# Summing the second sublayer's shift and scale over partitions: one-column TensorE products, or VectorE block transposes with small transfers

## Chip, core and metric

The kernel runs on one core of one Trainium2 chip. The metric is the device time of one execution in microseconds (us), the median of several runs. A profiled execution has a time of its own, and its instructions are counted from the first to the last (the span).

## What is computed

The reference is one post-norm layer of a streaming encoder over 512 tokens of width 1024, with two sublayers. Each sublayer's input is a layer norm that is shifted and scaled by vectors made from a condition `c` of width 1024:

```python
c_act = jax.nn.silu(c)
mod = c_act @ w_ada[l] + b_ada[l]
sh_t, sc_t, gt_t, sh_f, sc_f, gt_f = jnp.split(mod, 6, axis=-1)
h = _modulate(x, sh_t, sc_t)          # _layer_norm(x) * (1 + sc) + sh
y = _token_mixer(h, ...)              # pooling, latent attention, spatial gating; gates; w_o
x = _layer_norm(ALPHA * x + gt_t[:, None, :] * y) * ln_t_g[l] + ln_t_b[l]
h = _modulate(x, sh_f, sc_f)          # the vectors that this change is about
y = _conv_ffn(h, ...)
x = _layer_norm(ALPHA * x + gt_f[:, None, :] * y) * ln_f_g[l] + ln_f_b[l]
```

The change concerns only how `sh_f` and `sc_f`, 1024 numbers each, get their last sum.

## The kernel before

Activations stand transposed in SBUF: eight tiles of 128 channels by 512 tokens. Every large product is made of float32r matmuls of 128x128 by 128x512 with each operand split in a high and a low part. `chunk` loads one 128x1024 piece of weights, ScalarE casts it to the high part (L92, tiles such as `wbh`), VectorE subtracts to get the low part (L93, `wbl`), and `mm_chunk` runs 16 products with the high part (L113, L114) and 8 with the low part (L116). High and low tiles have two buffers each, raw tiles three, and `chunk` prepares one piece ahead, so the cast for the piece after the next waits until TensorE has finished with the high part in use.

The modulation vectors are formed piece by piece during the mixer. `ada_piece(idx, k)` loads 128 rows of the matrix for vector `idx` (0: `gt_t`, 1: `sh_f`, 2: `sc_f`, 3: `gt_f`) in two halves `adar` and adds them, times the condition's value for each row, to two accumulators `acc` of 128x512 (L850, L852, on VectorE). After eight pieces `acc` holds, per output channel, 128 partial sums that lie on 128 partitions; they still have to be added over the partitions. `ada_cols` does this on TensorE: each of eight 128x128 blocks of `acc` is the stationary operand and a column of ones the moving one, so that the result lands as one column with channels on partitions (L879, tile `pmc`); VectorE adds the bias (L883) and, for the scale, one (L885). The results `shfc` and `scfc` are read by `second_modulation` (L1262 to L1270) when the second sublayer begins.

The program around this, in order: `uv_half(1, "v", ...)` (the second half of the gating branch's v, with the last four pieces of `sh_f`), then `ada_cols(1, ...)`, then the branch `merge(1, m)` for m = 0 to 7 with `v_stats` and `v_norm` hung behind the weight splits, then `gated(g)` for g = 0 to 7 with the pieces of `sc_f` (each `gated` ends with four small products `pz`, L1046), then `ada_cols(2, ...)`, four `gate(2, m)`, and `merge(2, m)` for m = 0 to 7, each of the first four followed by `gate(2, m + 4)`. In `merge(2, m)` VectorE forms `th` from the product (L414), GpSimd adds it to the merged tile `mg` (L417), and ScalarE and VectorE split that into `mgh` and `mgl` (L1080, L1081). GpSimd also multiplies six tiles `oraw` of the output projection by `gt_t` (L1077); these tiles share a pool of eight (`pt`) with `acc`, `adar` and `gt_t`. The output projection `project_out`, the norm, the second modulation and the gated MLP follow.

A scheduler sets the order of each engine's queue from the order in the program and from when buffers come free; `behind_split` (called with a function) holds that function's instructions behind the last low-part subtraction. SyncE's queue (SP) issues the loads, GpSimd's queue (POOL) issued none.

Of the kernel before, what the change touches and what calls it, by code (L numbers as in the profile page):

```python
# [8 lines left out]
F32 = mybir.dt.float32  # L9
# [3 lines left out]
ALU = mybir.AluOpType  # L13
AX = mybir.AxisListType

P = 128
S = 512
D = 1024
KT = 8
# [13 lines left out]
C_SHT, C_SCT, C_SHF, C_SCF = 8, 16, 24, 32  # L33
# [17 lines left out]
def trunk(ctx: ExitStack, tc: tile.TileContext, A, out):  # L51
    nc = tc.nc

    const = ctx.enter_context(tc.tile_pool(name="const", bufs=1))
# [2 lines left out]
    wp = ctx.enter_context(tc.tile_pool(name="wp", bufs=2))  # L57
    sm = ctx.enter_context(tc.tile_pool(name="sm", bufs=4))
    pp = ctx.enter_context(tc.tile_pool(name="pp", bufs=8, space=bass.MemoryType.PSUM))

    def ps(name):
        return pp.tile([P, 512], F32, name=name, tag="ps")

    def act_t(name, dt=F32R):
        return sb.tile([P, 512], dt, name=name, tag="act", bufs=48)
# [4 lines left out]
    def m_t(name, dt=F32):  # L70
        return sb.tile([P, 512], dt, name=name, tag="m", bufs=8)
# [4 lines left out]
    def pad_t(name, dt=F32):  # L76
        return pd.tile([P, 528], dt, name=name, tag="pad")

    def f(ap):
        return ap.bitcast(F32)  # L80
# [20 lines left out]
    def behind_split(work, *args):  # L101
        with tc.issue_after(last_lo[0]):
            work(*args)
# [6 lines left out]
    def mm_chunk(o, wh, wl, xh, xl):  # L110
        cs = [slice(k * P, (k + 1) * P) for k in range(KT)]
        for k, c in enumerate(cs):
            nc.tensor.matmul(o, wh[:, c], xl[k], start=k == 0, stop=False)  # L113
            nc.tensor.matmul(o, wh[:, c], xh[k], start=False, stop=False)  # L114
        for k, c in enumerate(cs):
            nc.tensor.matmul(o, wl[:, c], xh[k], start=False, stop=k == KT - 1)  # L116
# [39 lines left out]
    def row_tiles(r, alloc, name):  # L156
        ts = []
        for n in range(2):
            t = alloc(f"{name}{n}", F32)
            nc.sync.dma_start(  # L160
                out=t, in_=A["rows"][r : r + 1, n * 512 : (n + 1) * 512].broadcast_to([P, 512])
            )
            ts.append(t)
        return ts
# [3 lines left out]
    cols = const.tile([P, N_COLS], F32, name="cols")  # L168
# [4 lines left out]
    for t in range(TT):  # L173
        for n in range(2):
            x_load = (nc.scalar if t == 3 else nc.sync).dma_start(
                out=xs[t][n], in_=A["x"][t * P : (t + 1) * P, n * 512 : (n + 1) * 512]
# [4 lines left out]
    ones = const.tile([P, P], F32, name="ones")  # L181
# [180 lines left out]
    def chunk(key):  # L362
        if key not in plan:
            return wsplit(A[key[0]][key[1:]], D, key[0])
        i = used[0]
        assert plan[i] == key
        for j in (i, i + 1):
            if j < len(plan) and j not in split:
                split[j] = wsplit(A[plan[j][0]][plan[j][1:]], D, plan[j][0])
        used[0] += 1  # L370
        return split[i]
# [21 lines left out]
    def gate(b, m, pg=None):  # L393
        if pg is None:
            gh, gl = chunk(("wg", b * KT + m))
            pg = ps("pg")
            mm_chunk(pg, gh, gl, hT_hi, hT_lo)
        th = act_t(f"th{b}{m}", F32)
        nc.scalar.activation(th, pg, AF.Tanh, scale=0.5)
        return th  # L400
# [3 lines left out]
    def merge(b, m, bh, bl, th):  # L404
        yh, yl = chunk(("wb", b * KT + m))
        py = ps("py")
        mm_chunk(py, yh, yl, bh, bl)
        if b == 0:
            merged[m] = m_t(f"mg{m}")
            nc.vector.scalar_tensor_tensor(  # L410
                out=merged[m], in0=th, scalar=1.0, in1=py, op0=ALU.add, op1=ALU.mult
            )
        else:
            nc.vector.scalar_tensor_tensor(  # L414
                out=th, in0=th, scalar=1.0, in1=py, op0=ALU.add, op1=ALU.mult
            )
            nc.gpsimd.tensor_tensor(out=merged[m], in0=merged[m], in1=th, op=ALU.add)  # L417
# [160 lines left out]
    for t in range(TT):  # L578
# [4 lines left out]
        for dst, tab in ((tA, cosT), (tB, sinT)):  # L583
            nc.vector.tensor_tensor(
                out=dst[:, t, :].rearrange("p (a b) -> p a b", a=2), in0=src,
                in1=tab[:, t : t + 1, :].broadcast_to([P, 2, 32]), op=ALU.mult,
# [253 lines left out]
    ada_state = {}  # L840
# [16 lines left out]
    def ada_rows(idx, r, name):  # L857
# [13 lines left out]
            nc.vector.tensor_tensor(out=bias[n], in0=pg, in1=bias[n], op=ALU.add)  # L871
        return bias

    def ada_cols(idx, c0, one, name):
        acc = ada_state.pop(idx)
        dst = const.tile([P, KT], F32, name=name + "c")
        pm = ps("pmc")
        for j in range(KT):
            nc.tensor.matmul(  # L879
                pm[:, j : j + 1], acc[j // 4][:, (j % 4) * P : (j % 4 + 1) * P], ones[:, 0:1],  # L880
                start=True, stop=True,
            )
        nc.vector.tensor_tensor(out=dst, in0=pm[:, 0:8], in1=cols[:, c0 : c0 + 8], op=ALU.add)  # L883
        if one:
            nc.vector.tensor_scalar_add(out=dst, in0=dst, scalar1=1.0)  # L885
        return dst


    po_hi = [None] * KT
    po_lo = [None] * KT  # L890
# [50 lines left out]
    for g in range(4):  # L941
        if g % 2 == 0:
            wh, wl = chunk(("wpool", g // 2))
        for mo in range(2):
            m = 2 * g + mo
            pm = ps("pmx")
            for k in range(2):
                o = (g % 2) * 512 + k * 256 + mo * P
                c = slice(o, o + P)
# [8 lines left out]
    def uv_half(i, nm, hook=None):  # L958
        tiles = [act_t(f"{nm}{i}{t}", F32) for t in range(TT)]
        pu = [ps("pu") for _ in range(TT)]  # L960
        for q in range(4):
            wh, wl = chunk(("wsg", i, q))
            for rest in range(2):
                for t in range(TT):
                    ts_ = slice(t * P, (t + 1) * P)
                    for kk in range(2):
                        k = 2 * q + kk
                        c = slice(kk * 512, (kk + 1) * 512)
                        hh, hl = hT_hi[k][:, ts_], hT_lo[k][:, ts_]
                        if rest:  # L970
                            nc.tensor.matmul(pu[t], hh, wl[:, c], start=False, stop=k == KT - 1)
                        else:
                            nc.tensor.matmul(pu[t], hl, wh[:, c], start=k == 0, stop=False)
                            nc.tensor.matmul(pu[t], hh, wh[:, c], start=False, stop=False)  # L974
            if hook:
                hook(q)
        for t in range(TT):
            nc.scalar.activation(tiles[t], pu[t], AF.Gelu)
        return tiles
# [7 lines left out]
    v0 = uv_half(0, "v", lambda q: behind_split(ada_piece, 1, q))  # L987
    gt_t = ada_rows(0, 0, "gtt")
    v1 = uv_half(1, "v", lambda q: behind_split(v_second, q))
    shf = ada_cols(1, C_SHF, False, "shf")  # L990
    gsg = row_tiles(6, pt_t, "gsg")
    bsg = row_tiles(7, pt_t, "bsg")

# [16 lines left out]
        )  # L1010

    v_work = [[(v_stats,)]] + [[(v_norm, t, 0)] for t in range(4)]
    v_work += [[(v_norm, 0, 1), (v_norm, 1, 1)], [(v_norm, 2, 1)], [(v_norm, 3, 1)]]
    for m in range(KT):
        th = th1[m] if m < len(th1) else gate(1, m)
        merge(1, m, mx_hi, mx_lo, th)
# [10 lines left out]
    for n in range(2):  # L1027
        nc.gpsimd.affine_select(
            out=ws[n].rearrange("p (g t) -> p g t", g=4),
            in_=wsr[:, n * 512 : (n + 1) * 512].rearrange("p (g t) -> p g t", g=4),  # L1030
# [30 lines left out]

    for g in range(KT):
        gated(g)
    scf = ada_cols(2, C_SCF, True, "scf")
    th2 = {m: gate(2, m) for m in range(4)}
    mg_hi = []
    mg_lo = []
# [4 lines left out]
            nc.sync.dma_start(out=o_raw[k][n], in_=A["wo"][k, :, n * 512 : (n + 1) * 512])  # L1072
    for m in range(KT):
        merge(2, m, sg_hi, sg_lo, th2.pop(m))
        if m < 6:
            raw = o_raw[2 + m // 2][m % 2]
            nc.gpsimd.tensor_tensor(out=raw, in0=raw, in1=gt_t[m % 2], op=ALU.mult)  # L1077
        mh = act_t(f"mgh{m}")
        ml = act_t(f"mgl{m}")
        nc.scalar.activation(mh, merged[m], AF.Copy, scale=0.5)  # L1080
        nc.vector.scalar_tensor_tensor(  # L1081
            out=ml, in0=merged[m], scalar=0.5, in1=f(mh), op0=ALU.mult, op1=ALU.subtract
        )
        mg_hi.append(mh)
        mg_lo.append(ml)
        if m + 4 < KT:
            th2[m + 4] = gate(2, m + 4)


    lntg = row_tiles(2, act_t, "lntg")  # L1090
    lntb = row_tiles(3, act_t, "lntb")

# [231 lines left out]
    for t in range(TT):  # L1324
        x1[t] = [m_t(f"x1_{t}{n}") for n in range(2)]
        for n in range(2):
            nc.sync.dma_start(
                out=x1[t][n], in_=A["x"][t * P : (t + 1) * P, n * 512 : (n + 1) * 512]
# [41 lines left out]
    for i in range(NP):  # L1370
        half = []
        for v in range(2):
            m = 2 * i + v
# [4 lines left out]
            else:  # L1378
# [9 lines left out]
                out=t[:, 1:512], in0=pz[:, 0:511], scalar=cols[:, cc + 1 : cc + 2],  # L1388
                in1=t[:, 1:512], op0=ALU.mult, op1=ALU.add,
            )  # L1390
            nc.vector.scalar_tensor_tensor(  # L1391
                out=t[:, 2:512], in0=pz[:, 0:510], scalar=cols[:, cc : cc + 1],
                in1=t[:, 2:512], op0=ALU.mult, op1=ALU.add,
# [165 lines left out]
```

## Time and profile before

| quantity | us |
|---|---|
| median of 3 runs (lowest, highest) | 957.66 (957.44, 957.80) |
| span of the profiled execution | 956.3 |
| TensorE matmuls busy | 942.2 |
| VectorE busy | 584.9 |
| ScalarE busy | 380.3 |
| GpSimd busy | 284.1 |

The profiled execution's own time is taken as its span, 956.3 us; the median of the runs lies 1.4 us above that (launch and close of the program, which the span does not hold). In the rows below a timeline row is: start in us, duration in us, engine, line, operation, written tile and read tiles, shape, count, and in brackets the engine's idle time before the row with what ended it. PE is TensorE, PEld its weight loads, DVE VectorE, ACT ScalarE, POOL GpSimd, SPq the queue of SyncE. The granted TensorE clock is 0.999 of full speed.

### The profile page before, as it was taken

The page shows a single profiled execution, that of the slowest core. Times are in us where ns is not written, and L with a number is a line of the kernel's source. Part 1 is how long each engine was busy: PE and PEld are TensorE (multiplying, and loading weights), DVE is VectorE, ACT ScalarE, POOL GpSimd, SP SyncE. Part 2 cuts the span into 40 slices and gives each one's busy share as a digit, 9 for nine tenths or more (in the row PEclk, how much of TensorE's full clock was granted, in tenths as well). Part 3 has the DMA queues.
Part 4 walks back from the last instruction along what each step waited for, and adds up shares of the span by engine and source line. Part 5 has one row for each costly group of instructions (what it writes and reads, how often), then busy time and mean ns, then how long its engine had stood idle before and what let it go on. Part 6 is the DMA issues. An engine that isn't in the chain of part 4 may idle for free.

```text
span 956.3 us, 12108 instructions
## 1 busy us (share of the span) xinstructions
PE 942.2 (99%) x4556; PEld 795.5 (83%) x4556; DVE 584.9 (61%) x850; ACT 380.3 (40%) x623; POOL 284.1 (30%) x248
## 2 busy tenths in 40 slices
PE   7999999999999999999999999999999999999996
PEld 6988888888888888888888888988888888888885
DVE  7966767546786665567233589575565664623258
ACT  4575555533233322232322334644434444321121
POOL 4741121122440032202123713021111121756653
PEclk9999999999999999999999999999999999999999
DMA  9823202145436533554333540134334333432322
GB/s 324 318 72 100 62 31 83 45 132 154 135 111 216 181 118 109 181 182 141 124 110 114 165 162 24 60 118 131 110 119 140 115 119 102 129 114 88 91 86 89
DMA packets 46139, 119.72 MB, mean 125 GB/s; under 512 B 5504, under 2 KB 8960, under 8 KB 46080
## 3 DMA queue, kind: packets, MB, share of 16 engines
q1 hardware_dynamic: 45648, 118.39, 38.4%
q8 instruction: 36, 0.59, 0.2%
q10 hardware_dynamic: 432, 0.55, 0.2%
q14 instruction: 23, 0.19, 0.1%
HBM read 116.83 MB, written 2.10 MB: 124 GB/s over the span
## 4 chain that ended last, share of the span: by engine, by line
PE 86%; DMA 5%; DVE 5%; POOL 2%; issue 1%; ACT 1%; SPq 0%; POOLq 0%; DVEq 0%; ACTq 0%
PE pzu L114 7%; PE pzu L116 7%; PE pzu L113 7%; PE pg L113 4%; PE pg L114 4%; PE pg L116 4%; PE py L113 4%; PE py L114 4%; PE py L116 4%; PE pyd L1132 3%; PE pyd L1129 3%; PE pyd L1131 3%; DMA ada<-in_ada1p 2%; PE pu L114 2%; PE pu L113 2%; PE pu L974 2%
## 5 line engine op out<-in xcount | busy, mean ns | idle before, releaser
L93 DVE TENSOR_TENSOR wupl<-wup,wuph 128x1024 fp32r<-128x1024 f32 x38 | 47.8, 1257 | 71.8 <-PE pzu L116 45.9
L1098 POOL TENSOR_TENSOR d<-d,gtfb 128x512 f32<-128x512 f32 x44 | 73.7, 1697 | 38.1 <-DMA d<-in_wdn 36.5
L1402 POOL TENSOR_TENSOR zc<-zc 128x512 f32<-128x512 f32 x22 | 29.7, 1350 | 173.1 <-ACT zc L1401 130.8
L1103 DVE TENSOR_TENSOR dl<-d,dh 128x1024 fp32r<-128x1024 f32 x18 | 27.8, 1542 | 57.0 <-PE pyd L1129 51.9
L92 ACT CAST wuph<-wup 128x1024 fp32r<-128x1024 f32 x38 | 39.9, 1049 | 46.8 <-PE pzu L114 46.8
L417 POOL TENSOR_TENSOR mg<-mg,th 128x512 f32<-128x512 f32 x16 | 31.3, 1959 | 86.4 <-DVE th L414 86.4
L92 ACT CAST wbh<-wb 128x1024 fp32r<-128x1024 f32 x24 | 25.2, 1052 | 74.0 <-PE py L114 55.3
L852 DVE SCALAR_TENSOR_TENSOR ada<-adar,cact,ada 128x512 f32<-128x512 f32 x56 | 49.1, 907 | 1.8 <-DMA adar<-in_ada 1.8
L93 DVE TENSOR_TENSOR wgl<-wg,wgh 128x1024 fp32r<-128x1024 f32 x22 | 29.6, 1343 | 29.7 <-PE pg L116 14.9
L1102 ACT CAST dh<-d 128x1024 fp32r<-128x1024 f32 x18 | 18.9, 1052 | 62.5 <-PE pyd L1132 33.2
L1384 ACT ACTIVATE zc<-pzu,cols 128x512 f32<-128x512 f32 x44 | 34.1, 778 | 21.8 <-PE pzu L116 17.4
L93 DVE TENSOR_TENSOR wbl<-wb,wbh 128x1024 fp32r<-128x1024 f32 x24 | 30.6, 1275 | 14.9 <-ACT wbh L92 6.5
L771 POOL TENSOR_SCALAR pe<-pe,mx 128x128 f32<-128x128 f32 (+3 forms) x32 | 17.0, 533 | 69.3 <-DVE mx L770 52.4
L1387 DVE SCALAR_TENSOR_TENSOR zc<-pzu,cols,zc 128x511 f32<-128x511 f32 x44 | 32.6, 744 | 4.2 <-ACT zc L1384 4.2
L92 ACT CAST wgh<-wg 128x1024 fp32r<-128x1024 f32 x22 | 23.3, 1058 | 25.6 <-PE pg L114 19.8
L1391 DVE SCALAR_TENSOR_TENSOR zc<-pzu,cols,zc 128x510 f32<-128x510 f32 x44 | 32.6, 745 | 0.8
L414 DVE SCALAR_TENSOR_TENSOR th<-th,py 128x512 f32<-128x512 f32 x16 | 11.0, 687 | 35.6 <-PE py L116 35.6
L1401 ACT ACTIVATE zc<-zc 128x512 f32<-128x512 f32 x22 | 13.9, 631 | 40.5 <-DVE zc L1391 40.4
L905 POOL TENSOR_TENSOR asum<-apad 128x527 f32<-128x527 f32 x8 | 12.3, 1544 | 54.6 <-ACT apad L900 28.0
L296 DVE SCALAR_TENSOR_TENSOR acc<-ada,cact,acc 128x256 f32<-128x256 f32 (+1 forms) x29 | 27.4, 944 | 1.2 <-DMA ada<-in_ada1p 0.3
L1077 POOL TENSOR_TENSOR oraw<-oraw,gttb 128x512 f32<-128x512 f32 x6 | 10.5, 1775 | 47.3 <-DMA oraw<-in_wo 47.3
L1098 POOL TENSOR_TENSOR o<-o,gttb 128x512 f32<-128x512 f32 x10 | 17.4, 1757 | 13.5 <-DMA o<-in_wo 7.7
(1473 smaller groups left out, 3088.4 us busy)
## 6 DMA issues: line engine op xcount, KB each, us to landing
wup<-in_wup SPq DMA_DIRECT2D x44, 512.0 KB, 3.6
adar<-in_ada SPq DMA_DIRECT2D x64, 256.0 KB, 4.1
wb<-in_wb SPq DMA_DIRECT2D x24, 512.0 KB, 3.6
wg<-in_wg SPq DMA_DIRECT2D x22, 512.0 KB, 3.6
d<-in_wdn SPq DMA_DIRECT2D x22, 512.0 KB, 3.6
ada<-in_ada1p SPq DMA_DIRECT2D x24, 256.0 KB, 4.9
wa<-in_wa SPq DMA_DIRECT2D x8, 512.0 KB, 3.6
wsg<-in_wsg SPq DMA_DIRECT2D x8, 512.0 KB, 3.6
```

The source lines that it names most:

```text
L92: nc.scalar.copy(out=hi[:, :n], in_=raw[:, :n])
L93: ins = nc.vector.tensor_tensor(out=lo[:, :n], in0=raw[:, :n], in1=f(hi[:, :n]), op=ALU.subtract)
L113: nc.tensor.matmul(o, wh[:, c], xl[k], start=k == 0, stop=False)
L114: nc.tensor.matmul(o, wh[:, c], xh[k], start=False, stop=False)
L116: nc.tensor.matmul(o, wl[:, c], xh[k], start=False, stop=k == KT - 1)
L417: nc.gpsimd.tensor_tensor(out=merged[m], in0=merged[m], in1=th, op=ALU.add)
L852: nc.vector.scalar_tensor_tensor(out=acc[n], in0=src, scalar=cact[:, k : k + 1], in1=acc[n], op0=ALU.mult, op1=ALU.add,)
L1098: nc.gpsimd.tensor_tensor(out=halves[n], in0=halves[n], in1=gt[n], op=ALU.mult)
L1384: nc.scalar.activation(t, pz, AF.Identity, bias=cols[:, cc + 3 : cc + 4], scale=cols[:, cc + 2 : cc + 3])
L1387: nc.vector.scalar_tensor_tensor(out=t[:, 1:512], in0=pz[:, 0:511], scalar=cols[:, cc + 1 : cc + 2], in1=t[:, 1:512], op0=ALU.mult, op1=AL ...
L1391: nc.vector.scalar_tensor_tensor(out=t[:, 2:512], in0=pz[:, 0:510], scalar=cols[:, cc : cc + 1], in1=t[:, 2:512], op0=ALU.mult, op1=ALU.add,)
L1402: nc.gpsimd.tensor_tensor(out=val, in0=val, in1=gate, op=ALU.mult)
```

## The change

The sixteen one-column products are taken out. `ada_parts` instead transposes `acc` in 32x32 blocks on VectorE, so that the 32 partitions of a block come to lie along the free axis, and reduces them; what is left is, for each channel, four partial sums, one from each quarter of the partitions, spread over four groups of 32 partitions. They are written to a DRAM tile by one transfer and read back by four (one for each group of 32 channels), all issued by GpSimd, so that channels lie on partitions with four values each. `ada_cols` then reduces four values and adds the bias on VectorE. `ada_parts` for the shift stands behind the last `v_norm` in `merge(1, 7)`, for the scale in `merge(2, 1)`; the two `ada_cols` stand in `merge(2, 0)` and `merge(2, 5)`.

```diff
+    def ada_parts(idx, name):
+        acc = ada_state.pop(idx)
+        part = const.tile([P, 4, KT], F32, name=name + "p")
+        for n in range(2):
+            blocks = pad_t("adab")
+            nc.vector.transpose(out=blocks[:, :512], in_=acc[n])
+            nc.vector.tensor_reduce(
+                out=part.rearrange("p a j -> p j a")[:, 4 * n : 4 * n + 4, :],
+                in_=blocks[:, :512].rearrange("p (j a c) -> p j a c", a=4, c=32),
+                op=ALU.add, axis=AX.X,
+            )
+        bounce = dr.tile([P, 4, KT], F32, name=name + "d")
+        nc.gpsimd.dma_start(out=bounce, in_=part)
+        quarters = const.tile([P, 4, KT], F32, name=name + "q")
+        for a in range(4):
+            nc.gpsimd.dma_start(
+                out=quarters[32 * a : 32 * a + 32],
+                in_=bounce.rearrange("(q c) a j -> c q a j", c=32)[:, :, a, :],
+            )
+        ada_quarters[idx] = quarters
...
     def ada_cols(idx, c0, one, name):
-        acc = ada_state.pop(idx)
         dst = const.tile([P, KT], F32, name=name + "c")
-        pm = ps("pmc")
-        for j in range(KT):
-            nc.tensor.matmul(
-                pm[:, j : j + 1], acc[j // 4][:, (j % 4) * P : (j % 4 + 1) * P], ones[:, 0:1],
-                start=True, stop=True,
-            )
-        nc.vector.tensor_tensor(out=dst, in0=pm[:, 0:8], in1=cols[:, c0 : c0 + 8], op=ALU.add)
+        nc.vector.tensor_reduce(
+            out=dst, in_=ada_quarters.pop(idx).rearrange("p q j -> p j q"), op=ALU.add, axis=AX.X
+        )
+        nc.vector.tensor_tensor(out=dst, in0=dst, in1=cols[:, c0 : c0 + 8], op=ALU.add)
...
-    shf = ada_cols(1, C_SHF, False, "shf")
...
-    v_work += [[(v_norm, 0, 1), (v_norm, 1, 1)], [(v_norm, 2, 1)], [(v_norm, 3, 1)]]
+    v_work += [[(v_norm, 0, 1), (v_norm, 1, 1)], [(v_norm, 2, 1)], [(v_norm, 3, 1), (ada_parts, 1, "shf")]]
...
-    scf = ada_cols(2, C_SCF, True, "scf")
...
     for m in range(KT):
         merge(2, m, sg_hi, sg_lo, th2.pop(m))
+        if m == 1:
+            behind_split(ada_parts, 2, "scf")
+        if m == 0:
+            behind_split(ada_cols, 1, C_SHF, False, "shf")
+        if m == 5:
+            behind_split(ada_cols, 2, C_SCF, True, "scf")
```

How the queues change is seen at three places. First, VectorE's queue in `merge(1, 7)`, where `v` is normalised, `th` is the last product's gate and `wul` the first low parts of the `gated` stage. Before:

```order
L93 TENSOR_TENSOR wul<-wu,wuh 128x1024
L1005 SCALAR_TENSOR_TENSOR v_3217<-v_3217,mvv,gsg_3385 128x512
L1008 SCALAR_TENSOR_TENSOR v_3217<-v_3217,rsv,bsg_3389 128x512
L414 SCALAR_TENSOR_TENSOR th_3746<-th_3746,py 128x512
L93 TENSOR_TENSOR wul<-wu,wuh 128x1024
```

The same place in the changed program, whose lines stand one to twenty-seven lower:

```order
L94 TENSOR_TENSOR wul<-wu,wuh 128x1024
L1025 SCALAR_TENSOR_TENSOR v_3217<-v_3217,mvv,gsg_3376 128x512
L880 STREAM_TRANSPOSE adab<-ada_3074 128x512
L880 STREAM_TRANSPOSE adab<-ada_3075 128x512
L1028 SCALAR_TENSOR_TENSOR v_3217<-v_3217,rsv,bsg_3380 128x512
L881 TENSOR_REDUCE shfp<-adab 128x4x4 x2
L415 SCALAR_TENSOR_TENSOR th_3737<-th_3737,py 128x512
L94 TENSOR_TENSOR wul<-wu,wuh 128x1024
```

Two transposes and two reductions have moved in ahead of the gate `th` and of a low part `wul`.

Second, GpSimd's queue across the end of `merge(1)` and the start of `merge(2)`; `mg` rows are the sums of `merge`, `oraw` rows the products with `gt_t`. Before:

```order
L417 TENSOR_TENSOR mg_2925<-mg_2925,th_3746 128x512
L1077 TENSOR_TENSOR oraw_4347<-oraw_4347,gttb_3192 128x512
L1077 TENSOR_TENSOR oraw_4348<-oraw_4348,gttb_3194 128x512
L1077 TENSOR_TENSOR oraw_4351<-oraw_4351,gttb_3192 128x512
L1077 TENSOR_TENSOR oraw_4352<-oraw_4352,gttb_3194 128x512
L1077 TENSOR_TENSOR oraw_4355<-oraw_4355,gttb_3192 128x512
L1077 TENSOR_TENSOR oraw_4356<-oraw_4356,gttb_3194 128x512
L417 TENSOR_TENSOR mg_2356<-mg_2356,th_4246 128x512
L417 TENSOR_TENSOR mg_2444<-mg_2444,th_4279 128x512
```

The same queue in the changed program:

```order
L887 DMA shfd<-shfp 128x32
L418 TENSOR_TENSOR mg_2927<-mg_2927,th_3737 128x512
L890 DMA shfq<-shfd 32x4x8 x4
L1102 TENSOR_TENSOR oraw_4340<-oraw_4340,gttb_3194 128x512
L1102 TENSOR_TENSOR oraw_4341<-oraw_4341,gttb_3196 128x512
L1102 TENSOR_TENSOR oraw_4344<-oraw_4344,gttb_3194 128x512
L1102 TENSOR_TENSOR oraw_4345<-oraw_4345,gttb_3196 128x512
L418 TENSOR_TENSOR mg_2358<-mg_2358,th_4239 128x512
L887 DMA scfd<-scfp 128x32
L1102 TENSOR_TENSOR oraw_4348<-oraw_4348,gttb_3194 128x512
L1102 TENSOR_TENSOR oraw_4349<-oraw_4349,gttb_3196 128x512
L890 DMA scfq<-scfd 32x4x8 x4
```

The row that follows there is the sum `mg_2446` of m = 1: five transfers and the last two `oraw` products have moved in between the sums of m = 0 and m = 1. Those two `oraw` products come later because their tiles take the place of `acc`, which is now read until the transposes.

Third, ScalarE's queue behind the cast `wbh` of m = 2; `wgh` is the high part for gate 6, `mgh` the split of the sum of m = 1, `th` the tanh of gate 5, and the second `wbh` the high part for m = 3. Before:

```order
L92 CAST wbh<-wb 128x1024
L1080 ACTIVATE mgh_4464<-mg_2444 128x512
L92 CAST wgh<-wg 128x1024
L399 ACTIVATE th_4499<-pg 128x512
L92 CAST wbh<-wb 128x1024
```

The same rows in the changed program:

```order
L93 CAST wbh<-wb 128x1024
L93 CAST wgh<-wg 128x1024
L1105 ACTIVATE mgh_4474<-mg_2446 128x512
L400 ACTIVATE th_4509<-pg 128x512
L93 CAST wbh<-wb 128x1024
```

`mgh` of m = 1 has moved behind the cast for gate 6 and stands ahead of the tanh of gate 5 and the cast `wbh` for m = 3.

More of the change, by code (lines that the diff above doesn't have):

```diff
@@ L59, in trunk @@
     pp = ctx.enter_context(tc.tile_pool(name="pp", bufs=8, space=bass.MemoryType.PSUM))
+    dr = ctx.enter_context(tc.tile_pool(name="dr", bufs=1, space=bass.MemoryType.DRAM))
     def ps(name):
@@ L872, in ada_rows @@
         return bias
+    def ada_parts(idx, name):
[18 more added lines that the diff above has]
+        ada_quarters[idx] = quarters
+    ada_quarters = {}
     def ada_cols(idx, c0, one, name):
-        acc = ada_state.pop(idx)
         dst = const.tile([P, KT], F32, name=name + "c")
-        pm = ps("pmc")
-        for j in range(KT):
-            nc.tensor.matmul(
-                pm[:, j : j + 1], acc[j // 4][:, (j % 4) * P : (j % 4 + 1) * P], ones[:, 0:1],
-                start=True, stop=True,
-            )
-        nc.vector.tensor_tensor(out=dst, in0=pm[:, 0:8], in1=cols[:, c0 : c0 + 8], op=ALU.add)
+        nc.vector.tensor_reduce(
+            out=dst, in_=ada_quarters.pop(idx).rearrange("p q j -> p j q"), op=ALU.add, axis=AX.X
+        )
+        nc.vector.tensor_tensor(out=dst, in0=dst, in1=cols[:, c0 : c0 + 8], op=ALU.add)
         if one:
             nc.vector.tensor_scalar_add(out=dst, in0=dst, scalar1=1.0)
-        return dst
+        modulation[idx] = dst
+    modulation = {}
     po_hi = [None] * KT
@@ L1087, in trunk @@
             th2[m + 4] = gate(2, m + 4)
+    shf, scf = modulation[1], modulation[2]
     lntg = row_tiles(2, act_t, "lntg")
```

## Prediction

> **What bounds the kernel now.** I read the page's totals, then TensorE's waits, then the timeline where the products stand.
>
> ```profile
> span 956.3 us, 12108 instructions
> PE 942.2 (99%) x4556; PEld 795.5 (83%) x4556; DVE 584.9 (61%) x850; ACT 380.3 (40%) x623; POOL 284.1 (30%) x248
> ```
>
> ```profile
> PE lat L480 <- DMA x<-in_x: 5.5, 1, 5.5
> PE pth L1247 <- ACT xr L1234: 0.6, 1, 0.6
> ```
>
> TensorE is busy for all but 14.1 us, most of it at the start and after the last product; in between its one wait worth naming is 0.6 us, at the transposes that open the second modulation. The engine is the bound, so a product taken from it is worth its own time, unless something else becomes late.
>
> What the products cost is read from the starts of their neighbours, since ends are modelled:
>
> ```profile
> 336.97 0.39 PE L971 MATMUL pu<-wsgl,hT7h 128*128 128x512 f32 x1
> 337.20 1.84 PE L879 MATMUL pmc<-ones,ada 128*128 128x1 f32 x16
> 338.90 0.49 PE L113 MATMUL py<-mx0l,wbh 128*128 128x512 f32 x1
> 342.67 0.39 PE L116 MATMUL py<-mx0h,wbl 128*128 128x512 f32 x1
> ...
> 344.49 0.39 PE L113 MATMUL py<-mx0l,wbh 128*128 128x512 f32 x1
> 348.11 0.39 PE L116 MATMUL py<-mx0h,wbl 128*128 128x512 f32 x1
> ```
>
> ```profile
> 442.41 1.05 PE L1046 MATMUL pz<-ws,v 128*128 128x128 f32 x8
> 446.94 0.39 PE L116 MATMUL pu<-hT0h,wul 128*128 128x512 f32 x1
> 448.75 1.05 PE L1046 MATMUL pz<-ws,v 128*128 128x128 f32 x8
> 449.64 1.85 PE L879 MATMUL pmc<-ones,ada 128*128 128x1 f32 x16
> 455.12 0.39 PE L116 MATMUL pg<-hT0h,wgl 128*128 128x512 f32 x1
> ```
>
> In each place eight products show as 16 records. They begin at 337.20, where the next large product would have stood.
>
> **What is removed.** First place: from 337.20 to the first low-part product is 342.67 − 337.20 = 5.47 us; the same stretch of an undisturbed piece (344.49 to 348.11) is 3.62. The products cost 1.85 us, 0.15 of it as a slower restart of the large ones. Second place: from `pz` to the low part takes 455.12 − 448.75 = 6.37 us with them and 446.94 − 442.41 = 4.53 without, so 1.84. Together **3.69 us**, all on the engine that sets the end. The three small VectorE operations that go (8 numbers a partition) were off the path.
>
> **Does the gain reach the end?** The chain of waits leaves TensorE once:
>
> ```profile
> 520.56 1.83 PE py L116 x8
> 522.45 0.57 issue
> 523.02 1.56 DVE wbl L93
> ...
> 580.60 0.82 ACT xr L1234
> 581.47 1.58 PE pth L1247 x12
> ```
>
> Between 522 and 581 it runs over VectorE, GpSimd, ScalarE and loads, and 581 is where TensorE waited the 0.6 us. So for 59 us the gain counts only if this chain starts earlier too. Its head is the end of a `py` product, and the loads in it are released by weight splits that wait for TensorE. I take it to move along in full.
>
> **First ada_parts (merge 1, m = 7).** It lands in this part of VectorE's queue:
>
> ```profile
> 395.63 0.75 DVE L1008 SCALAR_TENSOR_TENSOR v<-v,rsv,bsg 128x512 f32<-128x512 f32 x1
> 399.17 0.69 DVE L414 SCALAR_TENSOR_TENSOR th<-th,py 128x512 f32<-128x512 f32 x1 [2.79 <-PE py L116]
> 399.77 1.22 DVE L93 TENSOR_TENSOR wul<-wu,wuh 128x1024 fp32r<-128x1024 f32 x1
> ```
>
> ```profile
> 409.02 1.81 PE pu L116 x8
> ```
>
> ```profile
> L765 DVE TENSOR_REDUCE mx<-sc 128x1 f32<-128x512 f32 x8 | 5.5, 683 | 0.2
> ```
>
> A reduction of 512 elements is in the trace: 0.68 us, two are 1.37. A block transpose is not. Its bounds are half as many elements (0.42, below) and a VectorE operation of twice as many slowed by GpSimd (2.04, below); I take 0.69, what 512 elements cost in the `th` row. The sum is 2.75 us (2.2 to 5.5) against 2.79 idle, so it fits. If it takes 5.5, `th` and `wul` move by 2.7 and end at 402.6 and 403.7; `wul` is wanted at 409.02. Cost: nothing, with 5 us left.
>
> ```profile
> 584.13 0.42 DVE L1277 TENSOR_TENSOR h2T1l<-h2f,h2T1h 128x256 fp32r<-128x256 f32 x1
> 450.12 2.04 DVE L93 TENSOR_TENSOR wgl<-wg,wgh 128x1024 fp32r<-128x1024 f32 x1 [0.25 <-ACT wgh L92]
> ```
>
> The five transfers stand on GpSimd's queue beside one sum:
>
> ```profile
> 399.94 2.20 POOL L417 TENSOR_TENSOR mg<-mg,th 128x512 f32<-128x512 f32 x1 [7.50 <-DVE th L414]
> 442.38 3.51 POOL L1077 TENSOR_TENSOR oraw<-oraw,gttb 128x512 f32<-128x512 f32 x2 [40.24 <-DMA oraw<-in_wo]
> ```
>
> After it the engine idles for 40 us, which hides the write, its landing and the four reads. The accumulators stay taken some 60 us longer, so the first load for `sc_f` moves on SP behind the `v_norm` step of m = 4, still three merges ahead of its first use. Cost: nothing.
>
> **Second ada_parts (merge 2, m = 1).** Here something does become late. I keep to the clock of before; all of it shifts alike.
>
> ```profile
> 484.39 1.23 DVE L93 TENSOR_TENSOR wgl<-wg,wgh 128x1024 fp32r<-128x1024 f32 x1 [1.13 <-PE pg L116]
> 489.77 0.69 DVE L414 SCALAR_TENSOR_TENSOR th<-th,py 128x512 f32<-128x512 f32 x1 [4.16 <-PE py L116]
> ```
>
> VectorE's 4.16 us of idleness takes the 2.75 us whole (485.6 to 488.4). The last two `oraw` loads now wait for the transposes: 486.3 and 487.0, landing 3.7 us later (row below), 490.0 and 490.7. GpSimd multiplies them in 3.52 us, until 493.5; the write of the sums, issued at 488.4, has landed by then even at 3.7 us. Then come four issues of reads, and only behind them the sum of m = 1:
>
> ```profile
> 456.48 3.52 POOL L1077 TENSOR_TENSOR oraw<-oraw,gttb 128x512 f32<-128x512 f32 x2 [3.17 <-DMA oraw<-in_wo]
> 490.60 2.14 POOL L417 TENSOR_TENSOR mg<-mg,th 128x512 f32<-128x512 f32 x1 [8.74 <-DVE th L414]
> ```
>
> ```profile
> oraw<-in_wo SPq DMA_DIRECT2D x6, 256.0 KB, 3.7
> ```
>
> ```profile
> 458.88 0.33 SPq L85 DMA_DIRECT2D wg<-in_wg  x1
> ```
>
> ```profile
> L133 POOL TENSOR_TENSOR rsv<-pw,neghalf 128x4 f32<-128x4 f32 x1 | 1.0, 1027 | 0.1
> ```
>
> No row shows what GpSimd needs to issue a transfer. Below stands an issue on SP, 0.33 us; above, a full tile's sum on GpSimd, 2.14. I take 1.03, a small software-like operation of that engine (the power). Four are 4.1 us (1.3 to 8.6), so the sum runs from 497.6 to 499.8 where it ended at 492.7. Behind it waits ScalarE:
>
> ```profile
> 492.78 0.63 ACT L1080 ACTIVATE mgh<-mg 128x512 fp32r<-128x512 f32 x1 [3.76 <-POOL mg L417]
> 495.21 0.60 ACT L399 ACTIVATE th<-pg 128x512 f32<-128x512 f32 x1 [0.76 <-PE pg L116]
> 498.84 1.05 ACT L92 CAST wbh<-wb 128x1024 fp32r<-128x1024 f32 x1 [3.02 <-PE py L114]
> ```
>
> ```profile
> 505.89 0.39 PE L113 MATMUL py<-sg0l,wbh 128*128 128x512 f32 x1
> ```
>
> `mgh` ends at 500.4, the tanh at 501.0, the cast `wbh` at 502.1 instead of 499.9. TensorE first reads it at 505.89: 3.8 us of cover left. VectorE's low part behind it is wanted 3.6 us later still. By m = 3 GpSimd, with 8.74 us idle per step, is level again, long before 522. With d for one issue, the cast ends at 493.5 + 4d + 2.14 + 0.63 + 0.60 + 1.05 = 497.9 + 4d, and TensorE stalls only when d passes 2.0. At 2.14 it would lose 0.6.
>
> **The two ada_cols.** Three or four VectorE operations on 8 to 32 numbers a partition, whose results are read only behind the transposes at 581, some 80 us after the last transfer: nothing.
>
> **The sum.** 956.3 − 3.69 = 952.6 us for the profiled execution; the median of the runs stands 1.4 above its span, so 957.66 − 3.69 = 953.97, **954.0**. New on the edges: the first transfers on GpSimd's queue might lengthen launch or close. No row prices that; what now lies outside the span is 1.4 us, so I allow 0 to 1.4 and take 0. On the other side the 0.6 us wait at 581 may shrink to nothing.
>
> **Rivals.**
> *VectorE holds up the issues.* Where VectorE and GpSimd work at once, one gets slower: `wgl` takes 2.04 at 450.12 beside the `oraw` products and 1.23 at 484.39 alone. If each of the four issues waited for a VectorE operation of 1.23, that adds 4.9 to the 4.1; the cast would end at 506.9, a stall of 1.0, and the time 955.0. Against it: VectorE is idle for most of 493.5 to 497.6 (one subtraction, at 495.3). The Trainium skill, "SBUF — State Buffer", section "SBUF: two separate sides", warns of this: GpSimd writes the descriptors of transfers it issues through a port that VectorE can lock, so such a transfer looks blocked while VectorE runs. No row of this case has such a transfer yet; only its neighbour, the slowed `wgl`, agrees.
>
> *The chain from 522 to 581 does not move.* Then TensorE runs 3.7 us ahead and gives it back at the `pth` wait: 957.7, no change. For it: the wait is there already. Against: the chain's head is a TensorE row. A longer launch or close that eats the gain ends at the same time.
>
> *Slower.* GpSimd's issues are so long that TensorE stalls for the cast at 505.89. The loss passes the gain from 4d − 8.0 = 3.7, d = 2.9 us; at 3.5 the stall is 6.0 and the time 960.0. For it: four in a row with nothing between. Against: that is more than any GpSimd row on a full tile in this stage.
>
> **How the numbers follow.** The full gain gets 0.73 (its own range 953.2, the wait at 581 gone and 0.2 of spread, to 954.9); the VectorE hold-up 0.08; no change 0.11; slower 0.08. A change of 0.2%, 1.9 us, is about the least that a measurement of this kernel can tell from none. Faster is 0.73 + 0.08 = 0.81, same 0.11, slower 0.08. The predicted time is 954.0. The range runs from 953.2 to 956.0, the full gain less 0.6 for issues at their upper bound and 1.4 at the edges; it leaves out the last two cases, 0.19.
>
> **What would show it.** Right: no `pmc` rows, `py` 0.23 us behind `pu` where 1.93 stood, TensorE about 938.5 us busy, and every later stage early by 3.7. The second place: `mg` of m = 1 some 7 us later against its `th`, ScalarE's cast for m = 3 some 2 us later, and no TensorE wait there. Wrong: a TensorE wait for `wbh` near 502 to 506, a longer wait at `pth`, or issues on GpSimd over 2 us each.

## The result, and the profile after

The changed kernel takes 954.15 us (median of 5 runs, 953.64 to 954.40) beside 957.66 us before (5 runs, 957.33 to 957.93). The ratio is 0.9961, with a 95% interval of 0.9950 to 0.9973: 3.5 us less, where 3.69 was forecast. On another chip the same kernel took 953.85 us beside 957.83, ratio 0.9958 (0.9945 to 0.9970).

The page of the changed kernel, its totals and the one queue that is new:

```profile
span 952.1 us, 12075 instructions
PE 938.9 (99%) x4524; PEld 792.6 (83%) x4524; DVE 594.2 (62%) x860; ACT 380.5 (40%) x623; POOL 290.7 (31%) x258
...
q0 software_dynamic: 320, 0.07, 0.0%
```

TensorE has 32 records fewer and is busy for 3.3 us less; VectorE and GpSimd have ten instructions more each. TensorE is still the bound. All its waits (total, count, longest):

```profile
PE lat L481 <- DMA x<-in_x: 5.3, 1, 5.3
PE pqn L107 <- ACT wqk2h L121: 0.2, 1, 0.2
PE sc L759 <- DVE PTl L122: 0.2, 1, 0.2
```

The row of 0.6 us for `pth` is gone, and no new one has come. The two profiled spans differ by 956.3 − 952.1 = 4.2 us, which is more than the 3.69 of the products; this vanished wait can make up the difference. The timeline at the two places of the products:

```profile
337.21 0.39 PE L992 MATMUL pu<-wsgl,hT7h 128*128 128x512 f32 x1
337.44 0.39 PE L114 MATMUL py<-mx0l,wbh 128*128 128x512 f32 x1
...
341.06 0.39 PE L117 MATMUL py<-mx0h,wbl 128*128 128x512 f32 x1
...
447.15 1.05 PE L1066 MATMUL pz<-ws,v 128*128 128x128 f32 x8
451.68 0.39 PE L117 MATMUL pg<-hT0h,wgl 128*128 128x512 f32 x1
```

`py` stands 0.23 us behind `pu`, and the stretches are 341.06 − 337.44 = 3.62 us and 451.68 − 447.15 = 4.53 us: just the lengths of the undisturbed ones before. Progress agrees: the last of these rows stood at 455.12, 3.44 us later (the stages ahead of the first place happened to run 0.24 later here than in the earlier trace, which makes it 3.68).

The added work at the first place, on VectorE and then GpSimd:

```profile
393.90 1.30 DVE L880 STREAM_TRANSPOSE adab<-ada 128x512 f32<-128x512 f32 x2
...
395.75 1.27 DVE L881 TENSOR_REDUCE shfp<-adab 128x16 f32<-128x512 f32 x2
397.56 0.69 DVE L415 SCALAR_TENSOR_TENSOR th<-th,py 128x512 f32<-128x512 f32 x1 [0.53 <-PE py L117]
...
400.47 2.20 POOL L890 DMA_DIRECT2D shfq<-shfd  x4
```

A block transpose costs about as much as a reduction, 0.65 us each here. Both pairs fit in the idle time ahead of `th`; 0.53 us of it is left. At the second place, VectorE, GpSimd, ScalarE, and TensorE's first read of the cast:

```profile
482.09 1.30 DVE L880 STREAM_TRANSPOSE adab<-ada 128x512 f32<-128x512 f32 x2
483.31 1.24 DVE L881 TENSOR_REDUCE scfp<-adab 128x16 f32<-128x512 f32 x2
486.33 0.69 DVE L415 SCALAR_TENSOR_TENSOR th<-th,py 128x512 f32<-128x512 f32 x1 [1.78 <-PE py L117]
...
484.85 0.59 POOL L887 DMA_DIRECT2D scfd<-scfp  x1 [6.42 <-DVE scfp L881]
486.43 3.52 POOL L1102 TENSOR_TENSOR oraw<-oraw,gttb 128x512 f32<-128x512 f32 x2 [1.00 <-DMA oraw<-in_wo]
489.90 2.18 POOL L890 DMA_DIRECT2D scfq<-scfd  x4
492.10 2.09 POOL L418 TENSOR_TENSOR mg<-mg,th 128x512 f32<-128x512 f32 x1
...
494.22 0.63 ACT L1105 ACTIVATE mgh<-mg 128x512 fp32r<-128x512 f32 x1 [3.21 <-POOL mg L418]
494.76 0.58 ACT L400 ACTIVATE th<-pg 128x512 f32<-128x512 f32 x1
495.40 1.05 ACT L93 CAST wbh<-wb 128x1024 fp32r<-128x1024 f32 x1
...
502.45 0.39 PE L114 MATMUL py<-sg0l,wbh 128*128 128x512 f32 x1
```

The queue on GpSimd is the forecast one: two `oraw` products, four issues, and only then the sum of m = 1. But four issues take 2.18 us, 0.55 each. The cast `wbh` ends at 496.45 and is read at 502.45: 6.0 us of cover, as before the change (499.89 to 505.89).

### The profile page after: what moved, and what is told of

Its sections match the earlier page's. It is cut to its first block, busy times and chain, and to the rows that moved or that the text cites. A ratio compares the mean times of both kernels' runs of the same rounds, so it can differ in the third digit from the quotient of the medians.

```text
span 952.1 us, 12075 instructions
## 1 busy us (share of the span) xinstructions
PE 938.9 (99%) x4524; PEld 792.6 (83%) x4524; DVE 594.2 (62%) x860; ACT 380.5 (40%) x623; POOL 290.7 (31%) x258
## 4 chain that ended last, share of the span: by engine, by line
PE 97%; DVE 1%; DMA 0%; POOL 0%; issue 0%; ACT 0%; POOLq 0%; SPq 0%; ACTq 0%
PE pzu L117 7%; PE pzu L114 7%; PE pzu L115 7%; PE py L115 5%; PE py L114 5%; PE py L117 5%; PE pg L114 4%; PE pg L115 4%; PE pg L117 4%; PE pyd L1158 3%; PE pyd L1155 3%; PE pyd L1157 3%; PE lat L527 2%; PE pu L114 2%; PE pu L115 2%; PE pu L995 2%
```

## The experiments

**The theory**: the gain is TensorE's time of the 16 products, and all that is added is hidden, at the second place behind 6 us of cover. **Its rivals**: the moved work gives or takes part of the gain; the cover isn't there; the first transfers on GpSimd's queue cost about 0.3 us outside the span; VectorE blocks GpSimd's issues. The first four runs shared one chip and 27 runs of the kernel before (957.83 us), the last four another and 12 runs (957.55).

**The changed kernel again.**

> The changed kernel again, as the yardstick for the others on this chip. Every theory: 953.6 to 954.4 us, 3.3 to 3.8 under the kernel before.

Measured: 953.85 us (953.38 to 954.16), in the range named; the gain is 3.98, just over the 3.8 named for it. In this execution a wait is left where the chain returns to TensorE. The waits, then two steps of the chain that ended last:

```profile
PE pth L1273 <- ACT xr L1260: 0.2, 1, 0.2
```

```profile
516.90 1.83 PE py L117 x8
...
577.45 1.58 PE pth L1273 x12
```

Before, these steps stood at 520.56 and 581.47: the head of the chain moved by 3.66 us and its end by 4.02. So in this pair of executions the chain over VectorE, GpSimd, ScalarE and loads moved along in full.

**One half each.** The shift alone by transposes (`ada_products` is the old `ada_cols` with its eight products):

```
     for g in range(KT):
         gated(g)
+    ada_products(2, C_SCF, True, "scf")
...
-        if m == 1:
-            behind_split(ada_parts, 2, "scf")
...
-        if m == 5:
-            behind_split(ada_cols, 2, C_SCF, True, "scf")
```

> The shift by transposes and transfers, the scale by eight products as before. Theory (the gain is TensorE's time of the products, all that is added is hidden): half of it, 957.66 - 1.85 = 955.8 us, and a row of eight products is left at the second place alone. Rival (moved work gives or takes part of the gain: later oraw loads, a later sum of m = 1, both at the second place only): this kernel, which leaves the second place alone, differs from 955.8 by what that work is worth, by over 0.5 us. Rival (the first transfers on GpSimd's queue lengthen launch or close): 0.3 us of the gain is missing here, 956.1, and the time outside the span is 1.7 us instead of 1.4.

The scale alone:

```
     v1 = uv_half(1, "v", lambda q: behind_split(v_second, q))
+    ada_products(1, C_SHF, False, "shf")
...
-    v_work += [[(v_norm, 0, 1), (v_norm, 1, 1)], [(v_norm, 2, 1)], [(v_norm, 3, 1), (ada_parts, 1, "shf")]]
+    v_work += [[(v_norm, 0, 1), (v_norm, 1, 1)], [(v_norm, 2, 1)], [(v_norm, 3, 1)]]
...
-        if m == 0:
-            behind_split(ada_cols, 1, C_SHF, False, "shf")
```

> The scale by transposes and transfers, the shift by eight products as before. Theory: the other half, 957.66 - 1.84 = 955.8 us. Rival (moved work gives or takes part of the gain): off 955.8 by over 0.5 us, and the two halves do not add up to the whole. Rival (edges): 956.1 here too, so that the two halves together lose 0.6 us where the whole change loses 0.3: the gains of the halves sum to 3.1 beside 3.4 for both.

Measured: 955.93 us, ratio 0.9980 (0.9971 to 0.9989), a gain of 1.90; and 956.26 us, ratio 0.9984 (0.9975 to 0.9993), a gain of 1.57. Each half gives its own products' time within its interval (some ±0.9 us). The halves sum to 3.47 beside 3.98 for the whole; the 0.5 between them is less than these intervals can tell from nothing.

**The products put back, their results unread.**

```
+    def idle_products(idx):
+        acc = ada_state[idx]
+        pm = ps("pmc")
+        for j in range(KT):
+            nc.tensor.matmul(
+                pm[:, j : j + 1], acc[j // 4][:, (j % 4) * P : (j % 4 + 1) * P], ones[:, 0:1],
+                start=True, stop=True,
+            )
+        unread = const.tile([P, KT], F32, name=f"unread{idx}")
+        nc.vector.tensor_copy(out=unread, in_=pm[:, 0:8])
...
     v1 = uv_half(1, "v", lambda q: behind_split(v_second, q))
+    idle_products(1)
...
     for g in range(KT):
         gated(g)
+    idle_products(2)
```

> The changed kernel with the 16 products added again at their two old places, their results copied and read by nobody; the shift and scale still come from transposes and transfers. Theory: the products cost their 3.69 us again, so 957.6 to 957.9 us, the time of the kernel before, within 0.3. Rival (the later loads and the later sum of m = 1 cost something that the gain covers): over 958.2. Rival (part of the gain comes from the moved work): under 957.2. Rival (edges): 958.0, 0.3 over the kernel before, with 1.7 us outside the span.

Measured: 957.56 us (957.24 to 958.54), ratio to the kernel before 0.9999 (0.9990 to 1.0008). Here everything that was added runs as in the changed kernel, and with the products back the time is that of before: they cost 957.56 − 953.85 = 3.71 us, where 3.69 was read from the starts of their neighbours. (The interval is some ±0.9 us wide, so an agreement to 0.02 is in part luck.) The timeline shows them in their old places:

```profile
337.54 0.39 PE L1003 MATMUL pu<-wsgl,hT7h 128*128 128x512 f32 x1
337.76 1.84 PE L912 MATMUL pmc<-ones,ada 128*128 128x1 f32 x16
...
449.32 1.05 PE L1078 MATMUL pz<-ws,v 128*128 128x128 f32 x8
450.21 1.84 PE L912 MATMUL pmc<-ones,ada 128*128 128x1 f32 x16
455.68 0.39 PE L117 MATMUL pg<-hT0h,wgl 128*128 128x512 f32 x1
```

The second stretch is 455.68 − 449.32 = 6.36 us, as before; the first, up to the low-part product at 343.24, is 343.24 − 337.76 = 5.48. Against the undisturbed 4.53 and 3.62 the products take 1.83 + 1.86 = 3.69 us in this trace too. The unchanged time excludes that the added work costs or gives more than about 0.9 us.

**GpSimd held up.** Is the cover at the second place real, and how large?

```
-            nc.gpsimd.dma_start(
+            ins = nc.gpsimd.dma_start(
...
+        if idx == 2:
+            with tc.issue_after(ins.ins):
+                nc.gpsimd.tensor_tensor(
+                    out=pad_t("hold")[:, :32], in0=ones[:, :32], in1=ones[:, :32], op=ALU.pow
+                )
...
+            if m == 2:
+                cast_behind[:] = [mgh1, tanh_last[0]]
```

The last lines make the next cast wait, in ScalarE's order, for `mgh` of m = 1 and the tanh behind it.

> The changed kernel with one extra power of 128x32 on GpSimd behind the four reads of the scale and ahead of the sum of m = 1; ScalarE's cast wbh for m = 3 is tied behind the split of that sum, as it runs in the changed kernel. D is the extra operation's duration in the profile, guessed at 4 us from the 128x1 and 128x4 powers. Theory (TensorE reads the cast 6.0 us after it ends): a stall of D - 6.0 where D is over 6, so none at 4: the changed kernel's time within 0.4 us. Rival (the cover isn't there, each us of GpSimd at this place shows): D us slower, some 4.

Measured: 953.97 us (953.88 to 954.30). Timeline of GpSimd, ScalarE and TensorE:

```profile
491.62 6.24 POOL L901 TENSOR_TENSOR hold<-ones 128x32 f32<-128x32 f32 x1
...
500.16 1.04 ACT L96 CAST wbh<-wb 128x1024 fp32r<-128x1024 f32 x1
...
501.94 0.39 PE L119 MATMUL py<-sg0l,wbh 128*128 128x512 f32 x1
```

The power took 6.24 us, not the guessed 4, yet the time did not move: the cast ends at 501.20, 0.74 us ahead of its reader. (Of the 6.0 us it used 5.3, less than 6.24, mainly since the sum of m = 1 ran faster, 1.27 us instead of 1.95, with VectorE idle beside it.) That rules out the rival without cover: it asked for 6 us. The same with 128 columns:

> The same with a power of 128x128, D guessed at 13 us. Theory: TensorE waits for wbh of m = 3 for D - 6.0, some 7 us, and the time is longer by that. Rival (no cover): D, some 13 us. Rival (something later in GpSimd's queue is reached first, or ScalarE's order changes): a wait of another size at another row.

Measured: 971.24 us (970.40 to 971.75), ratio 1.0142 (1.0127 to 1.0157). Waits, timeline, and the granted clock by stretch (the number ahead of the last two):

```profile
PE py L119 <- ACT wbh L96: 14.4, 1, 14.4
```

```profile
491.52 21.60 POOL L901 TENSOR_TENSOR hold<-ones 128x128 f32<-128x128 f32 x1
...
516.49 0.79 PE L119 MATMUL py<-sg0l,wbh 128*128 128x512 f32 x1 [14.43 <-ACT wbh L96]
517.08 0.63 PE L120 MATMUL py<-sg0h,wbh 128*128 128x512 f32 x1
517.50 0.63 PE L119 MATMUL py<-sg1l,wbh 128*128 128x512 f32 x1
...
520.82 0.39 PE L119 MATMUL py<-sg5l,wbh 128*128 128x512 f32 x1
```

```profile
514.00:518.00 4.00, 1.51 (x4) 1.23 (x5) 2.61 (x3) 3.62 (x6) 1.57 (x2) 0.50 0.14 42
518.00:522.00 4.00, 4.00 (x14) 3.18 (x13) 1.43 (x2) 0.40 (x1) 0.00 (x0) 0.66 0.77 260
522.00:526.00 4.00, 4.00 (x19) 3.34 (x18) 0.67 (x2) 1.05 (x1) 0.00 (x0) 1.00 0.25 91
```

The wait stands at the named row, the cast `wbh`. D is 21.60, so the expectation was 15.6; 14.4 came, and 0.7 of the difference is the faster sum again (1.24 us). The span of the profiled execution grew by more, 968.7 − 952.3 = 16.4 over the changed kernel's profile above (this execution was the shortest of the four; by the medians of this chip the power of 128 columns costs 971.24 − 953.97 = 17.3 over that of 32). The other 2.0 us are the restart. Behind the wait most products start 0.43 us apart instead of 0.23, at a granted clock of 0.50, and full speed is back only after 520: the ten intervals from 516.49 to 520.82 take 4.33 us, where ten of 0.23 take 2.3. The Trainium skill, "TensorE: Matmul & The Clock Gate", section "Part 1: The HAM clock gate", says just this: half rate after idleness, full rate after some 3.4 us of work; the trace agrees, with about 4 us.

**The transfers on SyncE's queue.**

```
-        nc.gpsimd.dma_start(out=bounce, in_=part)
+        nc.sync.dma_start(out=bounce, in_=part)
...
-            nc.gpsimd.dma_start(
+            nc.sync.dma_start(
```

> The changed kernel with its ten new transfers issued by SyncE instead of GpSimd. Theory (all the added work is hidden): the changed kernel's time within 0.3 us, GpSimd's sum of m = 1 about 2.7 us earlier. Rival (the first transfers on GpSimd's queue cost 0.3 us at launch or close): 0.3 us faster than the changed kernel, with 1.4 us outside the span. Rival (the loads that stand behind on SyncE's queue, which waits for the sums, come late): slower, with a TensorE wait for a weight.

Measured: 954.51 us (953.50 to 955.12), ratio 0.9967 (0.9956 to 0.9979), beside 953.97 for the 32-column hold-up on the same chip: 0.5 over it where 0.3 was allowed, within what these runs scatter. The 0.3 us of the edges do not exist: the profiled run is 954.05 with a span of 952.3, 1.75 apart, though GpSimd issues nothing; and the kernel before has 957.49 beside 955.8, 1.69 apart. The sum of m = 1 is early as expected, and no wait came up:

```profile
490.06 1.28 POOL L418 TENSOR_TENSOR mg<-mg,th 128x512 f32<-128x512 f32 x1
```

It ends 2.85 us earlier than in the changed kernel (491.34 beside 494.19). Yet the cast `wbh` for m = 3 starts at 495.44, where it started at 495.40 there: ScalarE idles 2.00 us ahead of it, until TensorE has done with the old high part. The transfers themselves land sooner (last number; the first row is of this kernel, the other two of the changed one):

```profile
scfq<-scfd SPq DMA_DIRECT2D x4, 4.0 KB, 1.8
```

```profile
shfq<-shfd POOLq DMA_DIRECT2D x4, 4.0 KB, 4.4
scfq<-scfd POOLq DMA_DIRECT2D x4, 4.0 KB, 3.5
```

From GpSimd the reads of the scale land after 2.1 us in the kernel with the products back and 2.3 in the one with the scale alone, so the difference varies. It is worth nothing here, where they are read tens of microseconds later; so this isn't a better version.

**VectorE busy beside the issues.**

```
+    def vector_copies():
+        spare = pad_t("spare")
+        for _ in range(8):
+            nc.vector.tensor_copy(out=spare[:, :512], in_=gt_t[0])
...
+        if m == 1:
+            behind_split(vector_copies)
```

> The changed kernel with eight extra VectorE copies of 128x512 in 32 bits, placed beside GpSimd's four reads of the scale. Theory: VectorE has room for them, the time stays within 0.5 us. What it tells of the hold-up: if a busy VectorE blocks the issues, they take over 1 us each where they took 0.55, and land later than 3.0 to 4.1 us; if it doesn't, both stay.

Measured: 954.25 us (953.89 to 954.78), no change. Timeline of GpSimd and of single copies, then the landing:

```profile
490.46 2.19 POOL L890 DMA_DIRECT2D scfq<-scfd  x4
492.65 1.38 POOL L418 TENSOR_TENSOR mg<-mg,th 128x512 f32<-128x512 f32 x1
...
489.28 1.51 DVE L1088 COPY spare<-gttb 128x512 f32<-128x512 f32 x1
490.83 1.55 DVE L1088 COPY spare<-gttb 128x512 f32<-128x512 f32 x1
492.41 0.49 DVE L1088 COPY spare<-gttb 128x512 f32<-128x512 f32 x1
492.93 1.39 DVE L1088 COPY spare<-gttb 128x512 f32<-128x512 f32 x1
...
496.76 0.42 DVE L1088 COPY spare<-gttb 128x512 f32<-128x512 f32 x1
```

```profile
scfq<-scfd POOLq DMA_DIRECT2D x4, 4.0 KB, 3.8
```

The issues take 0.55 us each as they did without copies. If anything, VectorE is the one that waits: a copy of 0.42 us takes up to 1.55. The four copies shown that overlap GpSimd's work end at 490.79, 492.38, 492.90 and 494.32, each 0.26 to 0.29 us behind the end of a GpSimd operation or issue (490.51, 492.10, 492.64 and 494.03). Only the first three overlap the issues, and none of them runs at its own speed as an issue begins, so this run doesn't show what a copy that is under way would do to an issue. The reads land after 3.8 us beside 3.2 and 3.5 in two profiles of the changed kernel; over all kernels without copies it is 2.1 to 3.5, so the copies can't be named as the reason.

## Why the prediction was right, point by point

- **The products, 3.69 us.** Right: 3.69 again by the starts in the trace with the products put back, and 3.71 by the medians, which are sure to some 0.9 us only. The size came from the distance between large products on either side with and without the small ones; the distance from the first small product to the next large one (338.90 − 337.20 = 1.70) would have missed the 0.15 us of slower restart.
- **The gain reaches the end.** Right: the chain's head moved by 3.66 us and its end by 4.02. That the wait at `pth` may vanish was left open; it is 0 in one profile of the changed kernel, 0.2 in another, 0.6 before. With the products back there is no such wait either, so its going isn't owed to the products alone; why its size varies stays open. Whether the 0.3 by which the second chip's gain exceeds 3.69 is this wait, the runs can't tell.
- **The block transposes.** Taken at 0.69 us, the row of a 512-element operation; the two pairs took 1.30 each, 0.65 an operation.
- **The order at the second place.** Right: the `oraw` products end at 489.95, which is 493.4 on the clock of before (3.44 added), forecast 493.5.
- **One issue on GpSimd, d = 1.03.** This term was mis-sized: 0.55. The nearest row was an issue on another queue (0.33, the lower bound), not a small computation on the same engine. With 0.55 the prediction's own formula, 497.9 + 4d, gives 500.1; the cast ended at 496.45 + 3.44 = 499.9, exactly where it ended before. So it was not late at all (a cast some 2 us later had been named as a sign), the sum of m = 1 was late by 4.9 us instead of 7, and the cover was 6.0 us instead of 3.8. The formula also leaves out a term. The cast can't start before TensorE has done with the old high part: before the change ScalarE idled 3.02 us for that, and with the transfers on SyncE the cast started at the same time although the sum was 2.85 us earlier. The late sum was taken up by this idle time and by the cast for gate 6, which now runs ahead of the sum; none of the 6.0 us was needed. The conclusion, no stall, stood with more room; the two hold-ups show that the cover is a number and where it ends.
- **The edges, 0 taken of 0 to 1.4.** Right. The 1.4 itself was no property of the chip: it compared one execution's span with the median of other runs. Run by run the difference is 1.66 to 1.86, for the kernel before as for the changed one.
- **The rivals.** *VectorE holds up the issues*: not seen, even with copies put beside them, though no copy was under way on its own as an issue began. The Trainium skill, "SBUF — State Buffer", section "SBUF: two separate sides", names just such copies, in 32 bits within SBUF, as what locks GpSimd out, and says that whichever of the two engines starts first holds the port that they share until its instruction is over. Here the issues stayed at 0.55 us and the copies ended 0.26 to 0.29 us behind GpSimd's work: the trace agrees with the second sentence, GpSimd being the holder, and doesn't show the first. *The chain doesn't move*: refuted by its two ends. *Slower from d = 2.9*: the row is 0.55; but the mechanism is real, and the 128-column hold-up shows the stall at the row that was named.

## What to carry to other kernels

Where one engine is busy for 99% of the span, small work taken from it is worth the distance that it opens between its neighbours. Putting it back with its results unread checks that price apart from all that was moved, as finely as the runs repeat. Work moved to other engines must be followed along the queue it joins, to the first thing that the bound engine reads behind it, and its cover counted in microseconds: here 6.0, of which four issues used none, because ScalarE had been waiting for TensorE ahead of the cast anyway. For an operation that the trace doesn't show, take bounds from several rows: here an issue (0.55 us) lay nearer to an issue on another engine (0.33) than to another operation of the same engine (1.03), while the block transpose (0.65) was met by another operation of the same engine and size (0.69). One case of each makes no rule.

## What the runs showed of the hardware that was not expected

- The same four reads of 4 KB cost 0.55 us each to issue from GpSimd and take 2.1 to 4.5 us to land (medians of four, over the profiles); from SyncE they cost 0.33 to 0.43 us and land after 1.8.
- A wait of 14.4 us on TensorE cost 16.4 in the profiled execution: the products behind it ran at a granted clock of 0.50 for about 4 us.
- GpSimd's power takes (21.60 − 6.24) / 96 = 0.16 us per column of 128 numbers.
- GpSimd's sum of 128x512 takes 1.24 to 1.28 us with VectorE idle beside it. Where it starts behind a 128x1024 subtraction on VectorE, it takes 1.67 to 2.14 us: in five profiles (before, two of the changed kernel, the scale alone, the products back) the sum of m = 1 ends 1.13 or 1.14 us behind the end of that subtraction, however long it took itself.
- Beside GpSimd's work a VectorE copy of 128x512 took up to 1.55 us instead of 0.42, while GpSimd's issues did not lengthen.
